# Moving half of the output projections' weight splits, the last differential head's units and the rotary copies

## The chip, the cores and the metric

The kernel runs on one core of a Trainium2 chip. The core has engines that run side by side, each with its own in-order stream of instructions: TensorE (PE) multiplies matrices, with its weight loads shown as PEld; VectorE (DVE), ScalarE (ACT) and GpSimd (POOL) work on tiles; SyncE (SP) mainly issues DMA transfers. They wait for each other by semaphores. The metric is the device time of one execution in microseconds (us); lower is better. A time is the median of several executions of the same program.

## The reference, cut to what matters

The whole program is a trunk of two layers over 1024 tokens of 1024 features, all in float32. Each layer is a token mixer and a gated MLP with a short convolution. Layer 0 mixes by differential attention (8 heads, two score maps each, partial rotary), layer 1 by multi-head latent attention, MLA (16 heads, with one rotary key that all heads share).

```python
for i in range(DEPTH):                       # DEPTH = 2
    h = rms_norm(x, attn_norm_g[i])
    if i % N_MIXERS == 0:
        x = x + diff_attention(h, ...)       # ends in: o.reshape(b, s, D_MODEL) @ w_o
    else:
        x = x + mla_attention(h, ...)        # ends in: o.reshape(b, s, ...) @ w_o
    h = rms_norm(x, ffn_norm_g[i])
    x = x + conv_ffn(h, ...)
return rms_norm(x, final_norm_g)
```

In MLA the score of a head is a product over 64 own features plus one over 32 rotary features, whose key `k_pe` is the same for all 16 heads:

```python
sc = (jnp.einsum('bqhd,bkhd->bhqk', qn, k_nope)
      + jnp.einsum('bqhr,bkr->bhqk', qp, k_pe)).astype(jnp.float32) * scale
```

## The kernel before

**Split operands.** Every float32 product is done as three products of rounded halves: an operand x is split into a high part (a rounding copy, `hi`, L123 to 127) and a low part (x minus the high part, `lo`, L129 and 130). `mm3` (L117 to 121) issues high times low, high times high and low times high, so three matmuls stand for one. `hi` runs on ACT (L127) unless DVE is named (L125); `lo` runs on DVE unless POOL is named. `fetch` (L132) starts a DMA of a raw block into the next place of a ring, and `split` (L138) makes the two parts of a block.

**Order.** The code is written as a program for all engines. When the kernel is built, a scheduler of the framework puts the instructions of each engine into an order of its own, by dependences and a model of durations; the engine then runs them in that fixed order. So an edit at one place can move instructions far from it.

**Attention.** Both mixers run in steps (`steps`, L277). A step t handles one pair of query blocks of one head. It issues the score matmuls of its own pair, then the "units" of the step (pieces of the q, k and v projections of a later head or of the other half of the tokens), the transposes and the value product of step t - 1, and its own softmax. In layer 0 (`diff_attention`, L307) there are 32 steps, four to a head. A unit is (head, which, half), which is 0 for Q, 1 for K and 2 for V; K and V of the second half of the tokens stand in a head's first step, Q in its second, and the next head's first halves follow. Units of layer 0 take one bank of PSUM, "u", in turn, and 24 matmuls each. The o of a finished head goes to DRAM (`o_d`, stored at L1464 in layer 0 and L1513 in MLA).

**Output projection.** `project_first` (L459) computes o times the first four row blocks of w_o for all eight token tiles and adds it to x; `project_rest`, after it, does the last four. Each piece of o is read back from DRAM (`project`, L443; the DMA at L448), split, and multiplied: two groups of 12 matmuls to a token tile. In layer 0 the first four token tiles put their groups into the one bank "u" and are added at L472, the rest use the two-bank tiles "S" and are added at L477. In layer 0 these raw pieces of o go through the same ring (the two halves of s13) as the raw weights.

**The weights of it.** `prefetcher`, in the body of the kernel, gives a function `step` that each step of the last head (layer 0), or of the last ten steps (MLA), calls: it splits the row blocks that were fetched by the last call, low parts by turns on POOL and DVE, and fetches the next two. `finish` does so until all eight are split, ahead of `project_first`. In layer 0 the split blocks go to s0 to s7.

**The rotary copies.** A key of MLA is held as a tile of 128 partitions, the lower 64 the head's own, the upper 64 the rotary part. There are four such tiles, used by turns. The rotary part is computed once into tile 0 (`rotary`), and copied to tiles 1, 2 and 3 by `share` (L1327, half a tile of tokens a call). In layer 1, tile 1's copies are made ahead of the steps, tiles 2 and 3 in the steps 1 and 2 (`prepare`, L1332); the odd tiles on DVE, tile 2 on ACT.

Further names of the profile: L248 is a transpose, L1403 and L1404 are the score matmuls of layer 0, L1418 its exponential, L1431 the difference of the two maps; L1487 is the exponential of MLA, L1507 and L1508 its value product, L1485 and L1486 its mask and maximum, L1493 and L149 the scaling of probabilities.

Of the kernel before, what the change touches and what calls it, by code (L numbers as in the profile page):

```python
# [18 lines left out]
P = 128  # L19
S = 1024  # L20
D = 1024
NT = S // P
KD = D // P
# [3 lines left out]
DA_HEADS = 8  # L27
# [29 lines left out]
class Trunk:  # L57
# [249 lines left out]
    def diff_attention(self, o_d, prefetch):  # L307
        nc, a = self.nc, self.a

        H = [[[self.at(f"s{4 * half + 2 * part + g}", [P, 4, 512], F32R) for g in range(2)] for half in range(2)] for part in range(2)]  # L310
        tab = self.at("s12", [P, 2, S])
        self.raw = self.ring(*self.cut("s13"))
        self.w = self.ring("s8", "s9", "s10", "s11")
        R = SimpleNamespace(
            k=self.ring("u0", "u1", "u2"), qh=self.ring("u3", "u4"), v=self.ring("u5", "u6", "u7"),
            P=self.ring("u8", "u9", "u10", "u11", "u12"), pT=self.ring("u13", "u14", "u15"),
            o=self.ring("h2", "h3"), fin=self.ring("h4", "h5", "h6", "h7"),
            rope=self.ring("h8", "h9", "h10", "h11"),
        )
# [12 lines left out]
        def split_w(h, which):  # L332
            if h < DA_HEADS:
                raw = raws.pop((h, which))
                w = self.w([P, 2, D], F32R)
                self.hi(w[:, 0, :], raw)
                self.lo(w[:, 1, :], raw, w[:, 0, :], nc.gpsimd)
                heads[h]["w", which] = w[:, 0, :], w[:, 1, :]


        def fetch_x(i):
            x = R.P([P, D])
            nc.sync.dma_start(x, a["x"][i * P : (i + 1) * P, :])
            return x

        def token_tile(i, x):
            r = self.rstd(x, self.big(), D)
            nc.vector.scalar_tensor_tensor(x, x, r, g, ALU.mult, ALU.mult)
            s = slice((i % 4) * P, (i % 4 + 1) * P)
            for kg in range(2):  # L350
                self.turn_blocks(x[:, kg * 512 : (kg + 1) * 512], lambda part: H[part][i // 4][kg][:, :, s])

        def unit(h, which, half):
            hd = heads[h]
            return self.da_unit(R, H, hd["w", which], which, half, hd, tab)

        xs = [fetch_x(0)]
        g = self.gain("s11", a["attn_norm_g"][0])
        xs += [fetch_x(1), fetch_x(2)]
        fetch_w(0, 1)  # L360
        xs += [fetch_x(3)]
        fetch_w(0, 0)
        nc.sync.dma_start(tab, a["rope_da"])
        split_w(0, 1)
        for i in range(4):
            token_tile(i, xs[i])
            if i == 1:
                self.load_constants()
        xs += [fetch_x(4), fetch_x(5), fetch_x(6)]
        fetch_w(0, 2)  # L370
        split_w(0, 0)
        self.run([unit(0, 1, 0)])
        split_w(0, 2)
        fetch_w(1, 1)
        self.run([unit(0, 0, 0)])
        for i in range(4, NT):
            if i + 3 < NT:
                xs += [fetch_x(i + 3)]
            token_tile(i, xs[i])
        self.run([unit(0, 2, 0)])  # L380

        def prepare(t):
            h, p = divmod(t, 4)
            if p == 0:
                split_w(h + 1, 1)
                fetch_w(h + 1, 0)
            if p == 1:
                split_w(h + 1, 0)
                fetch_w(h + 1, 2)
            if p == 2:  # L390
                split_w(h + 1, 2)
            if p == 3:
                fetch_w(h + 2, 1)
            if h + 1 == DA_HEADS:
                prefetch()

        def units(t):
            h, p = divmod(t, 4)
            todo = [[(h, 1, 1), (h, 2, 1)], [(h, 0, 1), (h + 1, 1, 0)], [(h + 1, 0, 0)], [(h + 1, 2, 0)]][p]
            return [unit(*u) for u in todo if u[0] < DA_HEADS]  # L400

        self.steps(lambda t: DaStep(self, R, *divmod(t, 4), heads, o_d), units, prepare, 4 * DA_HEADS)
# [53 lines left out]

        return into

    def project_first(self, W, o_d, os, x_src, at, early):  # L459

        nc = self.nc
        X = [None] * NT
        for q, pair in enumerate(self.PAIRS):
            for i in pair:
                X[i] = at(q, i)
                nc.sync.dma_start(X[i], x_src[i * P : (i + 1) * P, :])
                into = self.project(i, range(0, 4), W, o_d, os, self.raw)
                if q < early:
                    for b in (0, 512):
                        y = self.bank("u")  # L470
                        into(y, b)
                        nc.vector.tensor_add(X[i][:, b : b + 512], X[i][:, b : b + 512], y)  # L472
                else:
                    y = self.big()
                    for b in (0, 512):
                        into(y[:, b : b + 512], b)
                    nc.vector.tensor_add(X[i], X[i], y)  # L477
        return X

    def project_rest(self, W, o_d, os, X, at, x_d, g, junk, places, nat, more, begin):  # L480
# [752 lines left out]
    def mla_heads(self, cT, v_d, o_d):  # L1233
        nc, a = self.nc, self.a
        pairs = MLA_HEADS // 2
        heads = [dict() for _ in range(MLA_HEADS)]
        W, V, raws = {}, {}, {}
        w_places = [("u2", "u3"), ("u4", "u5")]
        v_ring, q_ring, t_ring = self.ring("s13", "s4"), self.ring("s1", "s10", "s5", "s9"), self.ring("h10", "h11", "h8")
        k_places, kT = ["s0", "s11", "s12", "s8"], []  # L1240
# [3 lines left out]
            P=self.ring("u6", "u7", "u8", "u9", "u12"), pT=self.ring("u0", "u1", "u10", "u11"), o=self.ring("h4", "h5", "h6", "h7"),  # L1244
# [82 lines left out]
        def share(j, half):  # L1327
            k_tiles(j + 1)
            s = slice(half * 512, (half + 1) * 512)
            self.hi(kT[j][64:128, :, s], kT[0][64:128, :, s], nc.vector if j % 2 else None)  # L1330

        def prepare(t):  # L1332
            p, u = divmod(t, 8)
            if t == 0:
                fetch_w(1)
            if t == 1:
                split_w(1)
                share(2, 0)
                share(3, 0)
            if t == 2:  # L1340
                share(2, 1)
                share(3, 1)
            for at, ahead, f in ((2, 1, fetch_v), (4, 1, split_v), (5, 2, fetch_w), (7, 2, split_w)):
                if u == at and p + ahead < pairs:
                    f(p + ahead)
            if t >= 4 * MLA_HEADS - 10:
                prefetch[0]()
# [171 lines left out]
def kernel_body(tc, a, out):  # L1519
    with ExitStack() as ctx:  # L1520
        k = Trunk(tc, ctx, a)
        nc = tc.nc
        k.constants()
        dram = lambda name, shape: k.dr.tile(shape, F32, name=name)
        o_d = [dram(f"o_d{l}", [KD, P, S]) for l in range(2)]
        v_d = dram("v_d", [KD, P, NT, P])
        x_d = [dram(f"x_d{l}", [S, D]) for l in range(3)]
        g_d = [dram(f"g_d{l}", [NF, P, S]) for l in range(2)]
        units = lambda *ids: [f"u{i}" for i in ids]
        slots = lambda *ids: [f"s{i}" for i in ids]  # L1530
        halves = lambda *ids: [f"h{i}" for i in ids]
# [10 lines left out]
            return [lambda: piece(0), lambda: piece(1)]  # L1542


        def prefetcher(w_o, W, places):

            raws = []

            def step():
                while raws:  # L1550
                    W.append(k.split(places[len(W)], raws.pop(0), nc.vector if len(W) % 2 else None))
                while len(W) + len(raws) < KD and len(raws) < 2:
                    i = len(W) + len(raws)
                    raws.append(k.fetch(w_o[i * P : (i + 1) * P, :], D))

            def finish():
                while raws or len(W) < KD:
                    step()

            return step, finish  # L1560


        W = []
        step, finish = prefetcher(a["da_w_o"], W, slots(*range(8)))
        k.diff_attention(o_d[0], step)
        finish()
        first = {}
# [3 lines left out]
                first[q] = k.cut(f"s{8 + q}")  # L1571
            return first[q][i // 4]

        X = k.project_first(W, o_d[0], k.ring(*k.cut("s12", 512)), a["x"], at, 2)
        k.raw = k.ring("u14", "u15")
        pl = SimpleNamespace(
            T=dict(B11=slots(0, 1), B21=slots(2, 3), B22=slots(8, 9), T1=slots(12, 13), T2=slots(10, 11), T3=slots(4, 5), T4=slots(6, 7)),
# [7 lines left out]
        more = SimpleNamespace()  # L1585
# [69 lines left out]
        k.raw = k.ring("u14", "u15")  # L1655
        heads = k.mla_input(W_in, hts, turns, v_d, lambda cT: k.mla_heads(cT, v_d, o_d[1]))
        W = []
        step, finish = prefetcher(a["mla_w_o"], W, slots(2, 3, 6, 7, 1, 10, 0, 11))
        heads.rest(step)
        finish()  # L1660
        places = iter(units(2, 3, 4, 5, 12, 13, 10, 11))
        X = k.project_first(W, o_d[1], k.ring(*halves(0, 1, 2, 3)), x_d[1], lambda q, i: k.at(next(places), [P, D]), 0)
        pl = SimpleNamespace(
            T=dict(B11=slots(4, 9), B21=slots(12, 8), B22=slots(5, 13), T1=slots(6, 7), T2=slots(2, 3), T3=slots(10, 11), T4=slots(0, 1)),
            w=units(6, 7, 9, 8, 2, 3), sums=halves(9, 10, 11, 3, 8, 0), tmp=halves(1, 2, 4, 5, 6, 7), u=units(0, 1, 12, 13), t=units(10, 11),
# [112 lines left out]
```

## Time and profile before

| what | value |
|---|---|
| median of 3 executions | 2463.72 us (2462.08 to 2464.77) |
| profiled execution | 2467.78 us |
| its span, first to last instruction | 2466.0 us |
| mean granted clock of TensorE | 0.991 |

The profile is of one execution, with every instruction's start and length. A page sums it up; views of it show the busy time of each engine by windows, the timeline of an engine with what released it, and groups of like instructions. Matmuls overlap, so a matmul's own length (some 0.39 us for 512 columns) is longer than the distance to the next. "Clock" is the share of its full clock that TensorE was granted in a stretch.

The places that the change touches lie in the span like this: the last head of layer 0 from about 450 us, the start of the MLA steps at about 1365 us, and the last ten of them from about 1600 us.

### The profile page before, as it was taken

The page shows a single profiled execution, that of the slowest core. Times are in us where ns is not written, and L with a number is a line of the kernel's source. Part 1 is how long each engine was busy: PE and PEld are TensorE (multiplying, and loading weights), DVE is VectorE, ACT ScalarE, POOL GpSimd, SP SyncE. Part 2 cuts the span into 40 slices and gives each one's busy share as a digit, 9 for nine tenths or more (in the row PEclk, how much of TensorE's full clock was granted, in tenths as well). Part 3 has the DMA queues.
Part 4 walks back from the last instruction along what each step waited for, and adds up shares of the span by engine and source line. Part 5 has one row for each costly group of instructions (what it writes and reads, how often), then busy time and mean ns, then how long its engine had stood idle before and what let it go on. Part 6 is the DMA issues. An engine that isn't in the chain of part 4 may idle for free.

```text
span 2466.0 us, 32632 instructions
## 1 busy us (share of the span) xinstructions
PE 2380.1 (97%) x11960; PEld 2014.0 (82%) x11960; DVE 1906.0 (77%) x3088; ACT 1299.6 (53%) x2428; POOL 642.5 (26%) x507
## 2 busy tenths in 40 slices
PE   7999999899999999999999999999999999999998
PEld 5888887788888888788899788887888888887886
DVE  6667776846888888899864877776378888888997
ACT  5677777744444444444444777776244444444443
POOL 5545554525100000000042566655340000000001
PEclk9999999899999999999999999999999999999999
DMA  4111111313222222543222111123222222227501
GB/s 158 40 35 44 35 35 44 124 60 120 70 93 77 86 77 93 194 163 125 83 88 68 52 40 39 39 66 113 95 91 79 86 77 89 82 81 277 167 5 77
DMA packets 95104, 213.91 MB, mean 87 GB/s; under 512 B 8672, under 2 KB 33888, under 8 KB 94816
## 3 DMA queue, kind: packets, MB, share of 16 engines
q1 hardware_dynamic: 86048, 184.56, 22.8%
q10 hardware_dynamic: 8896, 27.27, 3.0%
q8 instruction: 94, 1.54, 0.3%
q14 instruction: 66, 0.54, 0.1%
HBM read 159.37 MB, written 52.43 MB: 86 GB/s over the span
## 4 chain that ended last, share of the span: by engine, by line
PE 80%; DVE 7%; ACT 5%; issue 3%; POOL 2%; DMA 2%; SPq 0%; ACTq 0%; POOLq 0%; DVEq 0%
PE S L119 13%; PE S L120 13%; PE S L121 13%; PE b L119 8%; PE b L121 8%; PE b L120 8%; PE u L119 3%; PE u L120 3%; PE u L121 3%; PE b L248 2%; PE b L182 1%; ACT u L1418 1%; PE u L1508 1%; PE u L1507 1%; ACT u L127 1%
## 5 line engine op out<-in xcount | busy, mean ns | idle before, releaser
L163 POOL TENSOR_TENSOR st<-st,mhalf 128x1 f32<-128x1 f32 x56 | 32.5, 580 | 1305.9 <-DVE st L162 1302.0
L127 ACT CAST u<-h 128x512 fp32r<-128x512 f32 (+2 forms) x242 | 146.1, 619 | 283.1 <-DVE h L632 260.6
L119 PE MATMUL S<-s,u 128*128 128x512 f32 (+1 forms) x752 | 286.3, 381 | 1.7 <-DVE u L776 1.0
L121 PE MATMUL S<-s,u 128*128 128x512 f32 (+1 forms) x752 | 284.7, 379 | 0.0
L120 PE MATMUL S<-s,u 128*128 128x512 f32 (+1 forms) x752 | 284.7, 379 | 0.0
L119 PE MATMUL b<-s,u 128*128 128x512 f32 x588 | 231.6, 394 | 0.5
L120 PE MATMUL b<-s,u 128*128 128x512 f32 x588 | 229.8, 391 | 0.0
L121 PE MATMUL b<-s,u 128*128 128x512 f32 x588 | 229.7, 391 | 0.0
L689 DVE SCALAR_TENSOR_TENSOR u<-u,conv,u 128x1023 f32<-128x1023 f32 (+1 forms) x176 | 224.9, 1278 | 1.6 <-ACT u L685 1.6
L149 POOL TENSOR_TENSOR u<-u,st 128x384 f32<-128x384 f32 (+7 forms) x160 | 169.5, 1067 | 161.2 <-DVE st L1493 108.0
L119 PE MATMUL u<-s,s 128*128 128x512 f32 x448 | 183.1, 409 | 13.8 <-ACT h L416 6.7
L130 DVE TENSOR_TENSOR u<-b,u 128x512 fp32r<-128x512 f32 (+1 forms) x256 | 158.7, 631 | 38.9 <-ACT u L127 36.6
L121 PE MATMUL u<-s,s 128*128 128x512 f32 x448 | 177.4, 396 | 0.0
L120 PE MATMUL u<-s,s 128*128 128x512 f32 x448 | 177.0, 395 | 0.0
L127 ACT CAST s<-u 128x512 fp32r<-128x512 f32 (+4 forms) x197 | 123.5, 663 | 96.4 <-PE u L121 35.1
L119 PEld LDWEIGHTS S<-s,u 128*128 128x128 f32 x752 | 141.8, 189 | 29.8 <-issue 2.1
L120 PEld LDWEIGHTS S<-s,u 128*128 128x128 f32 x752 | 142.0, 189 | 26.1
L121 PEld LDWEIGHTS S<-s,u 128*128 128x128 f32 x752 | 142.0, 189 | 26.0
L127 ACT CAST u<-b 128x512 fp32r<-128x512 f32 (+1 forms) x256 | 133.9, 550 | 47.9 <-PE b L248 44.3
L692 ACT ACTIVATE u<-u 128x1024 f32<-128x1024 f32 x44 | 46.7, 1062 | 198.8 <-DVE u L689 198.8
L248 PE MATMUL b<-ident,u 128*128 128x128 f32 x864 | 138.5, 278 | 8.5 <-DVE u L130 5.7
L130 DVE TENSOR_TENSOR u<-h,u 128x512 fp32r<-128x512 f32 x166 | 114.1, 687 | 32.4 <-ACT u L127 31.5
(257 smaller groups left out, 6635.4 us busy)
## 6 DMA issues: line engine op xcount, KB each, us to landing
u<-in_ffn_up SPq DMA_DIRECT2D x88, 512.0 KB, 3.9
g_d<-u ACTq DMA_DIRECT2D x44, 512.0 KB, 2.6
u<-in_ffn_down SPq DMA_DIRECT2D x66, 256.0 KB, 5.3
u<-g_d SPq DMA_DIRECT2D x62, 256.0 KB, 4.6
s<-in_da_wqkv SPq DMA_DIRECT2D x24, 512.0 KB, 3.7
x_d<-u SPq DMA_DIRECT2D x16, 512.0 KB, 2.9
s<-x_d SPq DMA_DIRECT2D x8, 1024.0 KB, 9.2
u<-o_d SPq DMA_DIRECT2D x24, 256.0 KB, 2.9
```

Source lines behind the costliest of these rows:

```text
L119: mm(out, lh, rl, start=first, stop=False, skip_group_check=onto)
L120: mm(out, lh, rh, start=False, stop=False, skip_group_check=onto)
L121: mm(out, ll, rh, start=False, stop=last, skip_group_check=onto)
L127: self.nc.scalar.copy(out, src)
L130: (eng or self.nc.vector).tensor_sub(out, src, hi.bitcast(F32))
L149: self.nc.gpsimd.tensor_mul(x, x, s.to_broadcast(list(x.shape)))
L163: nc.gpsimd.tensor_tensor(r, s, self.mhalf, ALU.pow)
L182: self.nc.tensor.transpose(ps[:, k * P : (k + 1) * P], src[:, k * P : (k + 1) * P], self.ident)
L248: self.nc.tensor.transpose(ps[:, j * P : (j + 1) * P], probs[t][:, k : k + P], self.ident)
L689: nc.vector.scalar_tensor_tensor(t[half][:, back:], u[half][:, : S - back], w, t[half][:, back:], ALU.mult, ALU.add)
L692: nc.scalar.activation(t[0], t[0], AF.Silu)
L1418: nc.scalar.activation(e, sc[c], AF.Exp, bias=nm[:, c : c + 1], accum_out=l[:, c : c + 1])
```

## The change

Three edits. `prefetcher` splits only the first four row blocks ahead of `project_first`. `finish` then issues the DMAs of the other four into places of their own, which the attention's probabilities held (u10 to u13 in layer 0, u6 to u9 in layer 1), and `project_first` calls `rest`, one split with its low part on DVE, after each of the token tiles 0 to 3. In layer 0's last head, the units K, Q and V of the second half of the tokens stand in one step each, in this order. In MLA, all rotary copies run on ACT, and those of tiles 2 and 3 are asked for one half tile a step in the steps 3 to 6.

```diff
         def units(t):
             h, p = divmod(t, 4)
             todo = [[(h, 1, 1), (h, 2, 1)], [(h, 0, 1), (h + 1, 1, 0)], [(h + 1, 0, 0)], [(h + 1, 2, 0)]][p]
+            if h + 1 == DA_HEADS:
+                todo = [[(h, 1, 1)], [(h, 0, 1)], [(h, 2, 1)], []][p]
             return [unit(*u) for u in todo if u[0] < DA_HEADS]
...
-    def project_first(self, W, o_d, os, x_src, at, early):
+    def project_first(self, W, o_d, os, x_src, at, early, more):
...
                     nc.vector.tensor_add(X[i], X[i], y)
+                if i < 4:
+                    more()
         return X
...
         def share(j, half):
             k_tiles(j + 1)
             s = slice(half * 512, (half + 1) * 512)
-            self.hi(kT[j][64:128, :, s], kT[0][64:128, :, s], nc.vector if j % 2 else None)
+            self.hi(kT[j][64:128, :, s], kT[0][64:128, :, s])
...
             if t == 1:
                 split_w(1)
-                share(2, 0)
-                share(3, 0)
-            if t == 2:
-                share(2, 1)
-                share(3, 1)
+                k_tiles(4)
+            if 3 <= t < 7:
+                share(2 + (t - 3) // 2, (t - 3) % 2)
...
-        def prefetcher(w_o, W, places):
+        def prefetcher(w_o, W, places, later):
...
+            half = KD // 2
 
             def step():
                 while raws:
                     W.append(k.split(places[len(W)], raws.pop(0), nc.vector if len(W) % 2 else None))
-                while len(W) + len(raws) < KD and len(raws) < 2:
+                while len(W) + len(raws) < half and len(raws) < 2:
                     i = len(W) + len(raws)
                     raws.append(k.fetch(w_o[i * P : (i + 1) * P, :], D))
 
             def finish():
-                while raws or len(W) < KD:
+                while raws or len(W) < half:
                     step()
-
-            return step, finish
+                for i, place in zip(range(half, KD), later):
+                    raws.append(k.at(place, [P, D]))
+                    nc.sync.dma_start(raws[-1], w_o[i * P : (i + 1) * P, :])
+
+            def rest():
+                if raws:
+                    W.append(k.split(places[len(W)], raws.pop(0), nc.vector))
+
+            return step, finish, rest
...
-        step, finish = prefetcher(a["da_w_o"], W, slots(*range(8)))
+        step, finish, rest = prefetcher(a["da_w_o"], W, slots(*range(8)), units(10, 11, 12, 13))
...
-        X = k.project_first(W, o_d[0], k.ring(*k.cut("s12", 512)), a["x"], at, 2)
+        X = k.project_first(W, o_d[0], k.ring(*k.cut("s12", 512)), a["x"], at, 2, rest)
...
-        step, finish = prefetcher(a["mla_w_o"], W, slots(2, 3, 6, 7, 1, 10, 0, 11))
+        step, finish, rest = prefetcher(a["mla_w_o"], W, slots(2, 3, 6, 7, 1, 10, 0, 11), units(6, 7, 8, 9))
```

In layer 1 `project_first` is given `rest` in the same way.

More of the change, by code (lines that the diff above doesn't have):

```diff
@@ L1661, in kernel_body @@
         places = iter(units(2, 3, 4, 5, 12, 13, 10, 11))
-        X = k.project_first(W, o_d[1], k.ring(*halves(0, 1, 2, 3)), x_d[1], lambda q, i: k.at(next(places), [P, D]), 0)
+        X = k.project_first(W, o_d[1], k.ring(*halves(0, 1, 2, 3)), x_d[1], lambda q, i: k.at(next(places), [P, D]), 0, rest)
         pl = SimpleNamespace(
```

## The prediction

> **What bounds the kernel now.** I read the page first (span, engines, chain of waits), then the busy time by windows around the three places that the diff touches, then the timelines of TensorE and of the engine that released it at each gap.
>
> ```profile
> span 2466.0 us, 32632 instructions
> PE 2380.1 (97%) x11960; PEld 2014.0 (82%) x11960; DVE 1906.0 (77%) x3088; ACT 1299.6 (53%) x2428; POOL 642.5 (26%) x507
> PE 80%; DVE 7%; ACT 5%; issue 3%; POOL 2%; DMA 2%; SPq 0%; ACTq 0%; POOLq 0%; DVEq 0%
> ```
>
> TensorE is busy for 97% of the span and is 80% of the chain that ends last. The change adds no matmul, so it can only win back time in which TensorE sits idle or runs at a lower clock, and it can only lose time by making more of that. So the question is where such time lies. The windows (columns: length, busy us of PE, PEld, DVE, ACT, POOL with counts, granted clock, DMA share, GB/s) show it: the first three lie in layer 0's last head, the next two at the start of the latent attention (MLA), the sixth is its long middle, then come its last steps, and the last is a stretch of layer 1's output projection.
>
> ```profile
> 450.00:460.00 10.00, 7.40 (x24) 5.69 (x25) 8.64 (x14) 7.68 (x15) 2.55 (x2) 0.83 0.56 206
> 470.00:480.00 10.00, 6.30 (x43) 5.19 (x41) 9.80 (x14) 7.08 (x18) 7.75 (x6) 0.88 0.68 236
> 480.00:490.00 10.00, 8.25 (x26) 6.84 (x27) 8.34 (x14) 8.46 (x20) 7.51 (x5) 0.50 0.18 54
> 1360.00:1370.00 10.00, 5.63 (x29) 4.23 (x27) 9.76 (x11) 6.03 (x8) 6.55 (x4) 0.93 0.52 157
> 1370.00:1380.00 10.00, 9.24 (x40) 7.67 (x40) 8.12 (x19) 7.12 (x15) 5.06 (x4) 0.73 0.08 19
> 1400.00:1640.00 240.00, 234.14 (x1506) 208.52 (x1505) 190.76 (x466) 176.72 (x388) 151.66 (x121) 1.00 0.14 41
> 1640.00:1650.00 10.00, 8.04 (x42) 6.87 (x41) 8.01 (x18) 6.97 (x15) 5.67 (x6) 0.83 0.30 88
> 1660.00:1670.00 10.00, 8.66 (x56) 7.38 (x55) 8.58 (x20) 8.74 (x19) 9.75 (x7) 1.00 0.71 229
> 1670.00:1680.00 10.00, 8.87 (x59) 7.24 (x58) 8.46 (x21) 7.67 (x17) 7.49 (x7) 1.00 0.52 175
> 1680.00:1690.00 10.00, 8.27 (x54) 7.28 (x54) 7.11 (x18) 7.06 (x16) 8.43 (x5) 1.00 0.29 84
> 1725.00:1755.00 30.00, 30.00 (x134) 24.80 (x133) 7.43 (x7) 3.73 (x6) 7.56 (x6) 1.00 0.22 66
> ```
>
> The last row gives the price of a 512-wide matmul at full clock, 30.00/134 = 0.224 us. In 470 to 480 TensorE is busy for 6.30 of 10 us while DVE is busy for 9.80: there DVE is the bound. In 480 to 490 the granted clock is 0.50, so half of 8.25 busy us are lost as well. Counting idle time plus the share of the clock that is missing, the three windows lose at most (2.60+1.7)+(3.70+1.2)+(1.75+4.1) = 15.1 us, the MLA start (4.37+0.4)+(0.76+2.5) = 8.0. That is all that there is to win at these places.
>
> **Part 1: the second half of the projection's weights goes out of the last head.** In layer 0, four 128x1024 row blocks lose their split there. What TensorE and DVE do around it (start, length, engine, instruction, idle time before and its releaser):
>
> ```profile
> 478.36 0.69 PE L248 MATMUL b<-ident,u 128*128 128x128 f32 x2 [1.70 <-DVE u L1431]
> 479.98 0.76 PE L1403 MATMUL S<-u,h 128*128 128x512 f32 x1 [0.94 <-ACT u L1418]
> 486.04 0.80 PE L1403 MATMUL S<-u,h 128*128 128x512 f32 x1 [1.60 <-ACT u L1418]
> 496.26 0.48 PE L1403 MATMUL S<-u,h 128*128 128x512 f32 x1
> 472.88 2.02 DVE L130 TENSOR_TENSOR s<-s,s 128x1024 fp32r<-128x1024 f32 x1
> 485.40 2.10 DVE L130 TENSOR_TENSOR s<-s,s 128x1024 fp32r<-128x1024 f32 x1
> L130 POOL TENSOR_TENSOR s<-s,s 128x1024 fp32r<-128x1024 f32 x28 | 69.1, 2467 | 48.8 <-ACT s L127 35.3 <-issue 11.6 <-DVE st L1428 1.8
> L127 ACT CAST s<-s 128x1024 fp32r<-128x1024 f32 x32 | 33.8, 1055 | 25.3 <-PE u L121 19.8 <-DVE u L348 2.6 <-DMA s<-in_da_w_o 2.6
> 483.90 8.81 SPq L448 DMA_DIRECT2D s<-o_d  x4
> DMA to landing us min/median/max: 3.6/4.0/6.2
> ```
>
> Removed from this stretch: 4 casts on ACT (4 x 1.06 = 4.2 us), two low parts on DVE (2.02 + 2.10 = 4.1) and two on POOL (2 x 2.47 = 4.9). The gaps of 1.70, 0.94 and 1.60 us end on DVE and ACT, the engines that are relieved. There is a second effect. The raw blocks no longer pass through the ring from which the o pieces are read, so the reads that waited on SP until 483.90 are issued earlier, and in the order of the built instructions four of the projection's first groups (48 matmuls) instead of one (12) stand ahead of the score that starts at 496.26. They fill the gaps: 36 x 0.224 = 8.1 us of work that TensorE has on hand while it waited.
>
> **Part 2** goes with this: Q comes before V, one unit a step. Its 72 matmuls, its rotary and transposes are the same in number; what moves is where they stand, by up to one step. That Q's score follows sooner is worth at most the 1.1 us by which the score could come at 495.2 when the two DVE low parts before it are gone, less what stands in the ring. So the ideal is 8.1 + 1.1 = 9.2 of the 15.1 lost. DVE, though, stays near its bound (9.80 less 2.02 in the worst window), so I take 7.7.
>
> Added are four DMAs of 512 KB on SP, four casts on ACT and four low parts, now all on DVE. The blocks are needed by the projection's second half, which begins about 545, and are split by about 516 if each lands 4.0 us after its issue: 29 us of cover, without which they would cost 4 x (1.06 + 2.1) = 12.6. The place where they can hurt is the order on ACT: the cast of block 4 stands ahead of the casts of two o pieces. Its DMA is issued when the last transposes have read the place that it goes to, lands 4.0 us later, and the casts take 1.06 and about 0.6; TensorE has 36 narrow matmuls between (half-width products, 36 x 0.11 = 4.0). The next projection group waits 4.0 + 1.06 + 0.6 - 4.0 = 1.7 us. Bounds: 0 if the place comes free sooner, 3.4 if the wait brings half a clock dip too. Layer 0: -7.7 + 1.7 = **-6** (from -11, ideal plus the second half of the half-clock time, to -2, the DVE bound).
>
> The low parts go to DVE just when POOL makes those of the o pieces. In the last row below, such a part of 1024 took 2.25 us with POOL at work, and in the group's mean 1.32. The Trainium skill, "GPSIMD Engine Reference", section "1. Specifications", says that POOL shares its interface to SBUF with DVE where two inputs come from SBUF; that speaks against the change, and the trace agrees. By it the four parts cost 4 x 0.93 = 3.7 us more on DVE; the sum stays, since DVE has 22.6 of 30 us free in the projection's window.
>
> ```profile
> L130 DVE TENSOR_TENSOR s<-u,s 128x1024 fp32r<-128x1024 f32 x10 | 13.2, 1324 | 2.3 <-ACT s L127 2.3
> 1666.24 2.25 DVE L130 TENSOR_TENSOR s<-u,s 128x1024 fp32r<-128x1024 f32 x1
> ```
>
> **Part 1 in layer 1.** The same edit at the end of the MLA:
>
> ```profile
> 1641.14 1.05 ACT L127 CAST s<-u 128x1024 fp32r<-128x1024 f32 x1 [1.74 <-DMA u<-in_mla_w_o]
> 1643.53 0.50 PE L119 MATMUL S<-s,s 128*128 128x512 f32 x1 [1.71 <-ACT u L1487]
> 1668.97 0.36 PE L1507 MATMUL u<-u,s 128*128 128x256 f32 x1 [1.06 <-DVE st L1493]
> 1671.11 1.18 PE L248 MATMUL b<-ident,u 128*128 128x128 f32 x7 [0.45 <-POOL u L149]
> 1675.46 0.50 PE L119 MATMUL S<-s,s 128*128 128x512 f32 x1 [0.62 <-ACT u L1487]
> 1683.05 0.38 PE L1507 MATMUL u<-u,s 128*128 128x256 f32 x1 [0.96 <-DVE h L1511]
> ```
>
> At 1641.14 ACT, in order, waits 1.74 us for a weight's DMA with the exponentials of the next step behind it, and TensorE misses those for 1.71 us; the clock then falls to 0.83 in that window (10 x 0.17 = 1.7). In the built order that cast now stands behind two exponentials, so both go: 3.4. The four later stalls (1.06 + 0.45 + 0.62 + 0.96 = 3.1) lie among the splits of blocks 4 to 7, which leave. Together 6.5; other DVE work is late next and takes a part of it, so **-4.5** (bounds -1, if only half the first stall goes, and -7).
>
> The Trainium skill, "TensorE: Matmul & The Clock Gate", section "HAM oscillation — how this bites in real kernels", wants a gap of over some 3.4 us for the half clock. By that rule the dip at 1643 is not the gap's doing and the sum would be 1.7 less; the rows differ, with clocks of 0.83 and 0.50 behind gaps of 1.71 and 1.70.
>
> **Part 3: rotary copies at the MLA start.**
>
> ```profile
> 1365.30 1.04 ACT L127 CAST s<-s 64x1024 fp32r<-64x1024 f32 x1
> 1366.37 0.48 ACT L127 CAST u<-b 128x384 fp32r<-128x384 f32 x1
> 1364.98 3.40 DVE L125 CAST s<-s 64x1024 fp32r<-64x1024 f32 x2
> 1368.41 0.56 DVE L130 TENSOR_TENSOR u<-b,u 128x384 fp32r<-128x384 f32 x1
> 1369.03 0.58 PE L1507 MATMUL u<-u,s 128*128 128x256 f32 x1 [4.13 <-DVE u L130]
> ```
>
> TensorE's longest gap here, 4.13 us, ends on DVE's low part at 1368.41, which stood behind the two copies of 3.40 us. They leave DVE. In the built order ACT has three copies one behind the other where it had one, so its 384-wide cast comes 2 x 1.04 = 2.1 us later, at about 1368.5, unless what is before them also comes earlier; DVE's low part follows it. The copies are thus not really spread: the order of the instructions hoists them. Between 3.40 gained on DVE and the delay on ACT, and with the clock of 0.73 in the next window (2.5 us) partly won back, I take **-3** (bounds 0, ACT takes DVE's place in full, and -6, the gap goes with its dip).
>
> The change also reorders the instructions of all 64 MLA steps. Nothing is added there. The long middle window has 240 - 234.14 = 5.9 us idle at clock 1.00, so it cannot win over 5.9; I take 0, with ±4.
>
> **Sum.** -6 - 3 - 4.5 + 0 = -13.5. The profiled execution took 2467.78 us (span 2466.0 and 1.8 around it), 4.1 above the median of the runs shown: 2454.3 for it, and 2463.72 - 13.5 = **2450** for a median.
>
> **The rivals.**
>
> *The DVE and ACT chains stay the bound.* For it: DVE at 9.80 of 10 in 470 to 480, and 8.34 after. Then the projection's early matmuls fill gaps, but the last scores come no sooner. Layer 0 gives only -2, the MLA tail -2, the start -1.5: 2458.
>
> *The copies only change engines.* If ACT is as late as DVE was, the MLA start gives 0 and the rest stands: 2453. For it: the three copies stand back to back. Against it: DVE is at 9.76 of 10 in 1360 to 1370, ACT at 6.03.
>
> *More is won.* If early projection work also takes the place of the half-clock time in 480 to 490, layer 0 gives its -11, and the tail its -6: 2463.72 - 20 = 2444.
>
> *Slower: the new order of the MLA steps.* One mechanism: in the middle window a step's exponential or low part falls behind another step's on its engine, and TensorE stalls as at 1643.53, for 1.71 us and 1.7 of lower clock, 3.4 each. Four such stalls eat the 13.5, and more than that decide for slower; six cost 20.4 and give 2463.72 + 6.9 = 2471. For it: every engine's order is changed there. Against it: 1506 matmuls with 2.4% idle at clock 1.00, ACT at 74% and DVE at 79%.
>
> **How the numbers follow.** A measurement of this kernel can tell about 0.2%, 4.9 us. The forecast (2445 to 2455, its own range) has 0.50; copies that only change engines 0.13, which lies in that range as well; the chains that stay 0.17, of which 0.10 counts as faster (below 2458.8) and 0.07 as the same; more won 0.08; slower order 0.12, of which 0.02 ends within 0.2% and 0.10 above. So faster is 0.81, same 0.09, slower 0.10. The parts' bounds give -11 - 6 - 7 = -24 at the far end and -2 - 0 - 1 = -3 at the near one, that is 2440 to 2461; with a part of the middle's ±4 the range is 2438 to 2464, which leaves out most of the slower case.
>
> **What would show it.** Right: in layer 0 four projection groups before the last head's last scores, no clock of 0.50 over ten us, and the projection starting some 6 us sooner; at the MLA start a gap of about 1 to 2 us where 4.13 was; at 1640 no ACT wait on a DMA of a weight; the middle window as busy as now. Wrong: a TensorE gap that ends on a cast of blocks 4 to 7 of over 2 us, DVE or ACT at over 95% in the last head with the same gaps, new stalls among the MLA steps, or a second half of the projection that waits for a low part.

## The result and the profile after

The changed kernel takes 2442.51 us (median of 6, 2441.41 to 2444.52) where the kernel before took 2463.30 us (median of 6, 2462.08 to 2465.87). The ratio is 0.9911, with a 95% interval of 0.9901 to 0.9921: 20.8 us less, 0.9%. The forecast was 2450, its range 2438 to 2464.

The profiled execution took 2441.99 us. Its page:

```profile
span 2440.2 us, 32668 instructions
PE 2365.8 (97%) x11960; PEld 2003.9 (82%) x11960; DVE 1905.3 (78%) x3088; ACT 1303.3 (53%) x2432; POOL 630.4 (26%) x503
```

TensorE has the same 11960 matmuls. The windows of the changed kernel, chosen like those of before and moved with the shift (columns: length, busy us of PE, PEld, DVE, ACT, POOL with counts, granted clock, DMA share, GB/s):

```profile
450.00:460.00 10.00, 7.24 (x27) 5.43 (x26) 8.65 (x14) 7.69 (x14) 2.55 (x2) 0.83 0.46 157
470.00:480.00 10.00, 10.00 (x62) 8.92 (x61) 8.62 (x15) 7.25 (x23) 6.60 (x7) 1.00 0.54 184
480.00:490.00 10.00, 10.00 (x58) 8.59 (x57) 7.31 (x15) 8.80 (x19) 3.02 (x3) 1.00 0.10 28
1350.00:1360.00 10.00, 6.98 (x36) 5.21 (x34) 8.72 (x13) 8.60 (x12) 6.61 (x4) 1.00 0.47 150
1360.00:1370.00 10.00, 8.30 (x43) 7.14 (x44) 7.63 (x18) 7.93 (x18) 6.09 (x4) 0.83 0.13 43
1390.00:1630.00 240.00, 236.73 (x1536) 211.90 (x1535) 196.81 (x482) 180.90 (x400) 156.79 (x125) 1.00 0.15 43
1660.00:1670.00 10.00, 10.00 (x71) 9.19 (x71) 9.12 (x23) 7.85 (x18) 6.26 (x4) 1.00 0.12 28
1670.00:1680.00 10.00, 9.77 (x79) 9.20 (x78) 8.80 (x26) 8.67 (x21) 6.46 (x6) 1.00 0.24 67
```

From 470 to 490 TensorE is now busy throughout, at full clock, where it had 14.55 of 20 us and a clock of 0.50 in the second half. Four of the projection's groups of 12 matmuls now stand ahead of the score at 496.25, where one stood ahead of the score at 496.26; the last head's last score comes at 500.34, 5.0 us sooner. The window at 450 is about as it was. In the long middle of the MLA steps TensorE does 30 more matmuls in the same 240 us. The last windows are nearly full.

How far this moves the work is best read from the starts of the same instruction in both traces. I use four landmarks: the first exponential of MLA (L1487 before), the value products (L1507) at one sixteenth and at eleven sixteenths of their number, and the last value product. The differences between them give each stage's own change against the profile of before, in us. The medians come from four sessions, in which the kernel before itself read 2463.3 to 2465.4; kernels of different sessions are compared by their ratios to before.

| kernel | median | layer 0, to the first exponential | MLA start | middle | last steps | TensorE's loss in the middle |
|---|---|---|---|---|---|---|
| before | 2463.3 | 0 | 0 | 0 | 0 | 11.0 |
| changed | 2442.5 | -10.7 | -2.8 | -4.3 | -7.0 | 5.5 |
| part 1 alone | 2459.9 | -3.9 | 0.0 | +0.1 | -4.9 | 11.0 |
| part 2 alone | 2462.2 | -3.2 | -0.5 | 0.0 | -2.3 | 11.0 |
| part 3 alone | 2452.8 | +0.2 | -1.8 | -5.9 | -6.7 | 4.2 |
| parts 1 and 2 | 2453.1 | -10.5 | -0.8 | +0.1 | -6.4 | 10.9 |
| parts 1 and 3 | 2449.8 | -4.0 | -2.2 | -3.7 | -7.0 | 6.1 |
| changed, no early groups | 2456.5 | -4.8 | -0.2 | 0.0 | -6.0 | 10.9 |
| tile 1 on ACT, 2 and 3 on DVE | one time | -2.4 | -0.3 | +0.1 | -2.3 | 10.9 |
| tiles 1 and 2 on ACT, 3 on DVE | one time | -2.7 | -0.4 | +0.1 | -2.4 | 10.9 |
| changed, tile 3 on POOL, splits later | 2449.4 | -9.9 | -2.8 | 0.0 | -4.1 | 10.9 |
| changed, high parts on DVE | 2442.0 | -13.3 | -2.5 | -6.2 | -5.4 | 3.9 |
| changed, all eight tiles through u | 2453.2 | -2.7 | -2.7 | -4.2 | -6.6 | 5.5 |
| high parts on DVE, tiles 2 and 3 on POOL | 2444.2 | -9.0 | +1.5 | -9.3 | -5.4 | 2.3 |

The last column is worked out from the traces: for each matmul of the middle the distance to the next one's start, less the price of its width at full rate (0.2265 us for 512 columns, about 0.1 for 128), added up where it is over 0.1 us.

The profiled execution of before took 2467.78 us, 4.5 above its median, and the table shows where. Three kernels whose last steps stand in the very order of before (part 2 alone, and the two with other copies) show -2.3 to -2.4 in that column; the four that leave layer 0 alone, before among them, show 0, +0.2, -2.4 and -2.7 in the first, -1.2 in the mean. In the same order, TensorE stood at half clock for 23.9, 23.9, 20.5 and 13.7 us of their layer 0, which goes some way to explain the differences. Part 2 alone shows -0.5 at the MLA start, which it doesn't touch. Taken from these zeros, the changed kernel wins about 9.5 us in layer 0, 2.3 to 2.8 at the MLA start, 4.3 in the middle and 4.7 in the last steps, in all some 21, against 20.8 by the medians. The columns are good to one or two us only, since the order around a landmark is not the same in all kernels: priced by width, the changed kernel has 0.9 us less matmul work ahead of the first exponential than before, 0.4 less in the MLA start, 0.3 more in the middle and 1.7 more before the last value product.

The steps that the prediction named show in these lines. First two gaps of TensorE that are left (start, length, engine, instruction, idle time before and its releaser), then ACT around them, then DVE:

```profile
524.87 0.50 PE L121 MATMUL S<-s,s 128*128 128x512 f32 x1 [1.14 <-POOL s L130]
1360.24 0.39 PE L1509 MATMUL u<-u,s 128*128 128x256 f32 x1 [2.28 <-DVE h L1513]
```

```profile
521.38 1.05 ACT L127 CAST s<-u 128x1024 fp32r<-128x1024 f32 x1 [2.61 <-DMA u<-in_da_w_o]
1355.84 2.94 ACT L127 CAST s<-s 64x1024 fp32r<-64x1024 f32 x3
1358.80 0.48 ACT L127 CAST u<-b 128x384 fp32r<-128x384 f32 x1
1359.31 0.37 ACT L1512 COPY h<-u 64x256 f32<-64x256 f32 x1
```

```profile
525.30 1.85 DVE L130 TENSOR_TENSOR s<-u,s 128x1024 fp32r<-128x1024 f32 x1 [0.48 <-ACT s L127]
1359.79 0.40 DVE L1513 TENSOR_TENSOR h<-h,u 64x256 f32<-64x256 f32 x1
```

At 521.38 ACT waits 2.61 us for the DMA of block 4, the cast of an o piece is behind it, then POOL's low part, and TensorE misses it for 1.14 us. At 1355.84 the three rotary copies run one behind the other for 2.94 us; the copy of L1512 stands behind them, DVE's L1513 behind that, and TensorE waits 2.28 us. This is not the wait of 4.13 made shorter. That one stood ahead of the second value product, where 0.42 us are left; the 2.28 stand ahead of the third, which had no gap before.

The 3.40 us that the two copies took on DVE before are not their own cost either. One took 2.79 us, the other 0.69, and the long one ran beside this instruction of POOL:

```profile
1364.88 2.34 POOL L130 TENSOR_TENSOR u<-u,u 128x1024 fp32r<-128x1024 f32 x1 [0.46 <-ACT u L127]
```

### The profile page after: what moved, and what is told of

The parts are those of the page before. It is cut to its first block, busy times and chain, and to the rows that moved or that the text cites. A ratio compares the mean times of both kernels' runs of the same rounds, so it can differ in the third digit from the quotient of the medians.

```text
span 2440.2 us, 32668 instructions
## 1 busy us (share of the span) xinstructions
PE 2365.8 (97%) x11960; PEld 2003.9 (82%) x11960; DVE 1905.3 (78%) x3088; ACT 1303.3 (53%) x2432; POOL 630.4 (26%) x503
## 4 chain that ended last, share of the span: by engine, by line
PE 81%; DVE 7%; ACT 4%; issue 3%; DMA 2%; POOL 2%; SPq 0%; POOLq 0%; ACTq 0%; DVEq 0%
PE S L119 13%; PE S L120 13%; PE S L121 13%; PE b L119 8%; PE b L120 8%; PE b L121 8%; PE u L119 4%; PE u L120 3%; PE u L121 3%; PE b L248 3%; PE u L1510 1%; PE u L1509 1%; PE b L182 1%; ACT u L1420 1%; PE S L1405 1%
```

## The experiments

**The parts, alone and in pairs.** Each kernel takes the whole lines of the change that belong to its part and leaves the others as they were. Without part 3, for instance:

```diff
-                k_tiles(4)
-            if 3 <= t < 7:
-                share(2 + (t - 3) // 2, (t - 3) % 2)
+                share(2, 0)
+                share(3, 0)
+            if t == 2:
+                share(2, 1)
+                share(3, 1)
```

Part 1 alone, in both layers:

> Only part 1 (second half of the weights split beside the projection, both layers). The built order of the MLA steps up to the last ones is that of before. Theory (splits are what crowds the last head and the MLA tail): layer 0 wins about 7 of its 10 us and the tail about 8.5, in all -13 to -16 us against before. Rival (the unit order is what frees layer 0, and part 3's new order is what frees the tail): layer 0 wins 0 to 2, the tail 3 to 4, in all -3 to -6.

Measured: 2459.94 us against 2464.65, ratio 0.9980 (0.9971 to 0.9989), -4.7. A miss; the total is in the rival's range, -3 to -6. Layer 0 did win early on: the last add of the projection's first half came 12.1 us sooner than in the profile of before. Then it gave most of it back. TensorE of this kernel, followed by SP's DMA issues:

```profile
538.41 0.40 PE L1461 MATMUL b<-h,ones 128*128 128x512 f32 x1
550.85 0.80 PE L119 MATMUL S<-s,h 128*128 128x512 f32 x1 [6.79 <-ACT h L127]
```

```profile
544.14 0.33 SPq L1466 DMA_DIRECT2D o_d<-h  x1
545.90 6.63 SPq L448 DMA_DIRECT2D u<-o_d  x3
```

The projection's second half needs the o of the last head. That head's end is late: its sum of squares (L1461) runs at 538.41, its o is stored at 544.14 (before: 538.85) and read back from 545.90 on, and TensorE waits 6.79 us for the cast of it. The early projection work had filled the gaps of the last head, and the gap came back behind it.

Part 2 alone:

> Only part 2 (Q before V, one unit a step, in the last head of layer 0); MLA as before. Theory: as the eight splits stay in the head, it is within 2 us of before, and TensorE's gaps on DVE and the half clock near 480 stay. Rival: the order of the units alone wins 6 us or more, without those gaps.

Measured: 2462.16, ratio 0.9989 (0.9980 to 0.9997), -2.5. That is half a microsecond past the theory's 2 us: with eight splits in the head the order of the units is worth little. The gaps on DVE stay, as it said (2.63 us at 480.17), but the half clock near 480 does not: the clock is 1.00 from 470 to 490.

Part 3 alone:

> Only part 3 (rotary copies on ACT, asked for in steps 3 to 6); layer 0 as before. Theory: the MLA start wins 3.5 us and the middle up to 3, the last steps nothing: -3 to -6. Rival 1: the new order also frees the last steps, -10 or more. Rival 2: the middle's gain is noise of the order, -1 to -3.

Measured: 2452.78, ratio 0.9953 (0.9940 to 0.9965), -11.9. The theory falls and rival 1 holds: this part, whose edits lie in the first steps, wins 5.9 us in the middle and about 4.4 in the last steps, and only 1.8 at the place that it touches.

Parts 1 and 2:

> Parts 1 and 2 without 3. Theory (parts add, 1 and 2 help each other in layer 0): -15 to -18 against before, with the MLA start's gap of 4.1 us still there. Rival (the tail's gain needs part 3): -10 to -12, with stalls in the last ten MLA steps.

Measured: 2453.09, ratio 0.9953 (0.9939 to 0.9966), -11.6. The theory missed, and the total is the rival's, but not for the rival's reason: the last steps win nearly as much as with part 3 (-6.4 against -7.0), and what is missing is the middle (+0.1 against -4.3). Parts 1 and 2 alone add up to 7.2, so together they win 4.4 more; layer 0 shows it, -10.5 against -3.9 and -3.2. The MLA start has its old gap:

```profile
1358.63 0.39 PE L1511 MATMUL u<-u,s 128*128 128x256 f32 x1 [4.13 <-DVE u L130]
```

Parts 1 and 3, to see whether part 2 takes away the wait for the last head's o:

> Parts 1 and 3 without part 2 (K and V in one step, then Q). The middle's order is the changed kernel's. Theory (part 2 brings the last head's own end forward, without it the projection's second half waits for the store and the load of the last head's o, 6.8 us as in part 1 alone): 6 to 7 us slower than the changed kernel, a gap of 6 us or more released by a cast of o near 550. Rival (parts add, part 2 is worth its own 2.5): 2 to 3 slower, no such gap.

Measured: 2449.77, ratio 0.9937 (0.9923 to 0.9950), by the ratios 6.4 us slower than the changed kernel; layer 0 alone loses 6.7. The theory holds, and the wait is there again:

```profile
551.40 0.79 PE L119 MATMUL S<-s,h 128*128 128x512 f32 x1 [6.82 <-ACT h L127]
```

In the changed kernel, with Q in front, SP stores the last o and reads it back about 5 us sooner, and no TensorE gap stands there (whether Q ahead of V or one unit a step does it was not tried apart):

```profile
538.99 0.33 SPq L1466 DMA_DIRECT2D o_d<-h  x1
541.02 5.07 SPq L450 DMA_DIRECT2D u<-o_d  x2
```

**Early projection groups.** One argument of `project_first` says how many pairs of token tiles go through bank u. At 0 they use the tiles that the scores need too, and can't stand ahead of the last scores.

```diff
-        X = k.project_first(W, o_d[0], k.ring(*k.cut("s12", 512)), a["x"], at, 2, rest)
+        X = k.project_first(W, o_d[0], k.ring(*k.cut("s12", 512)), a["x"], at, 0, rest)
```

> The changed kernel, but layer 0's first projection groups use the two-bank tiles S (which the scores need too) in place of bank u, so that they can't stand ahead of the last scores; splits and unit order are the changed kernel's. Theory (the groups that stand ahead fill TensorE's gaps): layer 0 loses 6 to 9 us of its 10, gaps released by ACT and DVE are back between 470 and 505, the total is -11 to -15 against before. Rival (the relief of ACT and DVE alone does it): within 2 us of the changed kernel, -19 to -22.

Measured: 2456.45, ratio 0.9964 (0.9951 to 0.9977), -9.0, less than the theory's -11 to -15. Layer 0 loses 5.9 us of its 10.7, just below the forecast, and TensorE waits for ACT and DVE as before, though the splits are out of the way:

```profile
477.85 0.39 PE L119 MATMUL b<-u,u 128*128 128x256 f32 x1 [2.37 <-DVE u L130]
487.40 0.80 PE L1405 MATMUL S<-u,h 128*128 128x512 f32 x1 [2.22 <-ACT u L1420]
```

So the relief of DVE and ACT alone is the smaller half; the groups on hand fill the gaps. The total fell by more than layer 0 did, because the MLA steps of this kernel came out in the order of before: see below.

**All eight tiles through bank u** (4 in place of 2 in the same argument):

> The changed kernel with all eight token tiles of layer 0's first half through bank u (16 groups that can stand ahead of or between the last scores, where 8 did). The middle's order is the changed kernel's. Theory (TensorE has no long gap left in the last head after 460): nothing more is won there, -1 to +1 against the changed kernel. Rival (more groups ahead fill more): -2 to -3.

Measured: 2453.17, ratio 0.9950 (0.9938 to 0.9963), by the ratios 9.6 us slower than the changed kernel. Both expectations missed. With one bank for all, groups wait for the add of the one before (three TensorE gaps of 0.46 to 0.96 us, of which the changed kernel has the first), and then the second half's transposes wait, for longer than in the three together. Why they come late was not taken apart:

```profile
567.67 1.12 PE L182 MATMUL b<-ident,h 128*128 128x128 f32 x4 [3.92 <-POOL h L495]
```

**Order or load in the MLA steps.** Two kernels change only which engine copies which tile, against the kernel before:

```diff
-            self.hi(kT[j][64:128, :, s], kT[0][64:128, :, s], nc.vector if j % 2 else None)
+            self.hi(kT[j][64:128, :, s], kT[0][64:128, :, s], nc.vector if j > 1 else None)
```

> The kernel before with the copies of tile 1 on ACT, and those of tiles 2 and 3 on DVE: as many copies on DVE (4) and ACT (2) as before, in another built order of the MLA steps. Theory (the order alone decides the middle): time that TensorE loses over 0.1 us a matmul in the middle of the MLA steps, 11.0 us in every kernel with before's order, is another here, by 2 us or more either way. Rival (the load of DVE decides): 10 to 12.

> The kernel before with tile 1's copies on ACT, tile 3's still on DVE: half of the engine change of part 3, in a third order. Theory (order alone): the middle's loss is a number of its own, not midway between 11.0 and part 3's 4.2. Rival (load): 7 to 8.5. At the MLA start the gap of 4.13 us is under 1.5 in both, since one or no copy stands ahead of DVE's low part.

(The second has `j == 3` there.) One time each, 2462.32 and 2464.75, near before. Both lose 10.9 us in the middle. The load rival's number for the first came true and for the second didn't (7 to 8.5). The theory's condition was not met either: the middle of their built order turned out to be before's, row for row (1363 TensorE rows between the landmarks), so neither had an order of its own. And the gaps at the start are 3.99 and 3.53, not under 1.5: one copy on DVE is enough when it stands beside POOL (2.76 us in the second kernel).

```profile
1365.78 0.58 PE L1507 MATMUL u<-u,s 128*128 128x256 f32 x1 [3.53 <-DVE u L130]
```

What settles it is the last column of the table beside the built orders. Eight kernels have before's order in the middle, and all lose 10.9 or 11.0 us there, whatever engine makes the copies; among them the one without early groups, which has part 3 in full. The copies themselves can't act there: in every kernel they are over more than 20 us before the middle begins. The order of part 3 alone and of the kernel with high parts on DVE loses 4.2 and 3.9; that of the changed kernel 5.5, 5.5 and 6.1. The waits of TensorE in the middle (what waited, for whom: us, times, longest) of before, of the kernel without early groups, and of the changed kernel:

```profile
PE b L248 <- DVE u L130: 4.2, 8, 0.9
```

```profile
PE b L248 <- DVE u L130: 4.1, 8, 0.8
```

```profile
PE b L248 <- DVE u L130: 1.1, 2, 0.9
```

In before's order a transpose waits eight times, by turns 0.18 and 0.86 us, for a bank that a low part on DVE still reads; in the other orders it mostly doesn't. By the measure of the table's last column these waits are 5.6 of the 11.0 us before and 1.5 of the 5.5 in the changed kernel; the rest of the loss is spread over many small steps. Over the middle of both, of the kernel without early groups and of part 3 alone, TensorE is busy for 97.6% and 98.9% of the middle, and DVE does more in the second, not less:

```profile
1396.00:1607.00 211.00, 205.85 (x1328) 183.21 (x1327) 166.98 (x408) 155.24 (x342) 133.96 (x107) 1.00 0.13 38
```

```profile
1397.00:1609.00 212.00, 209.73 (x1369) 188.71 (x1367) 172.95 (x422) 160.54 (x351) 142.24 (x112) 1.00 0.13 38
```

The built orders show one thing more, by building alone (these two were not run). A kernel with only the spread of the copies over steps 3 to 6 has, on all five engines, the very order of before, and one with only the move to ACT has that of part 3. The scheduler hoists the copies wherever they are asked for.

**Attempts at more.** First tile 3's copies on POOL, and blocks 4 to 7 split after token tiles 4 to 7:

```diff
-            self.hi(kT[j][64:128, :, s], kT[0][64:128, :, s])
+            (nc.gpsimd.tensor_copy(kT[j][64:128, :, s], kT[0][64:128, :, s]) if j == 3 else self.hi(kT[j][64:128, :, s], kT[0][64:128, :, s]))
...
-                if i < 4:
+                if i >= 4:
                     more()
```

> The changed kernel with two further edits in separate places: tile 3's rotary copies on POOL, and the splits of blocks 4 to 7 after the token tiles 4 to 7 in place of 0 to 3. Theory: of the three copies of 2.94 us on ACT at the MLA start one or two leave, the gap of 2.28 us behind them falls under 1; the wait of 1.14 us at 524.87 in layer 0, behind block 4's cast, goes: -2 to -4 against the changed kernel, give or take 3 from the new order of the steps. Rival (POOL's copies delay its scaling of probabilities, and the blocks come late for the second half): 0 to +4.

Measured: 2449.36, ratio 0.9930 (0.9914 to 0.9947), by the ratios 4.7 us slower than the changed kernel, about the rival's +4, though the two intervals overlap. The middle fell back into before's order (4.3 us), the gap at the start was still 1.75, and block 4's cast was hoisted to where it had been, with the same 1.14 us of waiting behind it.

Then the high parts of blocks 4 to 7 on DVE, which takes that cast out of ACT's order by force:

```diff
-                    W.append(k.split(places[len(W)], raws.pop(0), nc.vector))
+                    raw, w = raws.pop(0), k.at(places[len(W)], [P, 2, D], F32R)
+                    k.hi(w[:, 0, :], raw, nc.vector)
+                    k.lo(w[:, 1, :], raw, w[:, 0, :], nc.vector)
+                    W.append((w[:, 0, :], w[:, 1, :]))
```

> The changed kernel, but the high parts of blocks 4 to 7 are made on DVE like their low parts, so that no cast that waits for a weight's DMA stands in ACT's order. Its MLA steps come out in the order of part 3 alone, whose middle lost 4.2 us. Theory: the wait of 1.14 us at 524.87 goes, the middle loses 4 to 4.5 in place of 5.5, DVE (under 50% busy there) takes the four copies (about 1.2 us each) without harm: -1 to -3 against the changed kernel, -22 to -24 against before. Rival (the adds that free bank u wait behind DVE's weights): a new gap of over 1 us released by the add, 0 to +2.

Measured: 2441.99, ratio 0.9909 (0.9894 to 0.9925). Against the changed kernel's 0.9911 that is no difference that can be told. The mechanism is as expected: no wait near 524.87, DVE waits for the weights instead, in time that it has, and the middle loses 3.9.

```profile
521.72 0.69 DVE L125 CAST s<-u 128x1024 fp32r<-128x1024 f32 x1 [1.97 <-DMA u<-in_da_w_o]
```

Last, the same with tiles 2 and 3 copied on POOL:

> The changed kernel with the high parts of blocks 4 to 7 on DVE and the rotary copies of tiles 2 and 3 on POOL (tile 1's on ACT). Its MLA steps have a fourth order, which shares 1133 of 1277 rows of the middle with part 3's alone. Theory: the middle loses 4 to 5.5 (order); at the MLA start the gap of 2.28 us behind ACT's three copies falls under 1, as ACT keeps one: -2 to -5 against the changed kernel, 2438 to 2441. Rival (POOL needs over 1.5 us a copy and holds up its scaling of the probabilities): a gap of over 1.5 us released by POOL at the MLA start, and no gain.

Measured: 2444.17, ratio 0.9918 (0.9904 to 0.9931). The middle's loss is the lowest of all, 2.3 us, but the MLA start is 4.3 us worse than the changed kernel's (+1.5 and -2.8 in the table). A part of both is work that moved: there is 1.5 us less of it in this middle than in before's and 0.7 more in the start than in the changed kernel's. POOL is not slow, two copies take 2.37 us; the gap only falls to 1.45, because DVE now has a maximum and a low part of its own ahead of the add that TensorE waits for. What else the start loses was not taken apart. POOL first, then DVE:

```profile
1357.27 2.37 POOL L1334 CAST s<-s 64x1024 fp32r<-64x1024 f32 x2
```

```profile
1359.41 1.09 DVE L1488 TENSOR_REDUCE st<-S 128x1 f32<-128x896 f32 x1
1360.41 0.55 DVE L130 TENSOR_TENSOR u<-b,u 128x384 fp32r<-128x384 f32 x1
1360.88 0.40 DVE L1513 TENSOR_TENSOR h<-h,u 64x256 f32<-64x256 f32 x1
```

No version beat the changed kernel beyond its interval.

## Why the prediction was right, and where its sizes were off

The sign, the range and three of the places held; the forecast's own band (2445 to 2455) was 2.5 us too high, and the rival "more is won" (2444) came closest. The fourth place, the middle, was put at nothing either way and gave a fifth of the gain; that it fell on the fast side was luck. Without it the total would lie at about 2447, inside the band.

- **Layer 0, -6 forecast, about -9.5 measured.** The term that was mis-sized is the shading of the ideal 9.2 to 7.7 because "DVE stays near its bound": DVE fell from 9.80 to 8.62 of 10 us and TensorE ran full, so the ideal was reached whole, as far as a column good to one or two us can tell. The wait behind block 4's cast, put at 1.7, is there with 1.14 us, through the chain that was described; that it is this cast is shown by the kernel without it on ACT.
- **What carries layer 0** was put wrongly between parts. Part 2 was given at most 1.1 us; taking it out costs 6.4. The prediction looked at the gaps before the last scores and not at what the last head's own end sets free: its o, which the second half of the projection reads back. With early groups ahead of it that end becomes the next bound, and Q in front brings it forward. The early groups themselves, priced at 8.1 for three more than before, are worth 5.9 in layer 0 by the kernel that has none ahead.
- **The cover of blocks 4 to 7** was put at 29 us. The second half began at about 541, and block 7's low part ended at 525.30 + 1.85 = 527.15: 14 us, still enough. Of the four low parts only this one, begun while POOL was at work, took 1.85; the others took 1.21 to 1.23. So the slowdown that the prediction took from the Trainium skill, "GPSIMD Engine Reference", section "1. Specifications" (VectorE and GpSimd share their interface to SBUF when a VectorE instruction has two inputs there), came to 0.6 us in place of 3.7.
- **The MLA start, -3 forecast, -2.3 to -2.8 measured,** of which 0.4 is work that moved. The first half of the mechanism held: the copies leave DVE, they are hoisted together, and ACT comes late behind them. The path from there was another. The cast at 1366.37 that the prediction delays is not the one that the low part at 1368.41 reads; that is the 384-wide cast before it, at 1363.38, which no copy holds up. So the gap of 4.13 all but went, to 0.42, and a new one came one value product later, behind DVE's add L1513 and ACT's copy L1512. That its 2.28 us lie near the forecast's "1 to 2" is luck. The two copies were read as 3.40 us of DVE's work; about 1.4 is theirs, as 0.69 is what the others took, and the rest is the time that one stood beside POOL. The rival in which ACT gives all of it back did not hold, though the kernel without early groups, with the same copies and a gap of 2.33, wins only 0.2 here, with 0.9 us more work ahead of its landmark; what else it loses is open.
- **The middle, 0 ± 4 forecast, -4.3 measured,** a little outside. The prediction said that every order changes there and gave it no sign. It bounded the gain by the 5.9 us idle of the window of 234.14 of 240 busy us. TensorE's loss by the distances was 11.0 in the 218 us between the landmarks, since a matmul's own length counts as busy, and it is longer than the distance that it needs; the last kernel brought it down to 2.3. The slower rival was the same idea with the other sign.
- **The last steps, -4.5 forecast, about -4.7 measured,** but not for the forecast's reason alone: part 1 by itself wins about 2.6 there, part 3's order by itself about 4.4, both together 4.7.

That the loss in the middle follows the order and not the load is shown by kernels of equal order with the copies on different engines, all of them over before the middle begins. Why the scheduler falls into one order or another after a distant edit is open: it was seen, not tried apart.

## What to carry to other kernels

Work that is moved ahead to fill an engine's gaps wins only if the chain that follows is not the next bound: look up who reads the result of the work that now stands behind it (here a store and a load of the last head's o, 6.8 us). Where a scheduler fixes the order, compare the built orders before explaining a difference: an edit can be nothing in the order (the spread over steps) or reorder steps far away (the copies' engine), and a stall that comes back at each step shows as a waiter with a count. A window at 97% busy can still hold several microseconds.

## What the hardware showed unexpectedly

Equal orders lose nearly equal time in the middle, where the clock is full in every kernel: the eight profiles with before's order agree within 0.1 us of 11. The two with part 3's order lose 4.2 and 3.9, the three with the changed kernel's 5.5, 5.5 and 6.1. So differences of about a microsecond in such a stretch can be read from one trace, smaller ones not.

The lower clock does not follow from the gap's length alone. The window from 450 to 460 has two gaps; with 1.31 and 1.44 us (high parts on DVE) the clock stayed 1.00, with 1.32 and 1.44 (changed) it fell to 0.83, which is half clock for 3.41 us in the trace. High parts on DVE, its window and its gaps:

```profile
450.00:460.00 10.00, 7.25 (x34) 5.78 (x34) 8.65 (x14) 7.68 (x15) 2.56 (x2) 1.00 0.47 159
```

```profile
451.33 0.50 PE L1405 MATMUL S<-u,h 128*128 128x512 f32 x1 [1.31 <-ACT u L1420]
453.96 0.50 PE L119 MATMUL u<-s,s 128*128 128x512 f32 x1 [1.44 <-DVE h L234]
```

The changed kernel's gaps there:

```profile
452.05 0.50 PE L1405 MATMUL S<-u,h 128*128 128x512 f32 x1 [1.32 <-ACT u L1420]
454.68 0.63 PE L119 MATMUL u<-s,s 128*128 128x512 f32 x1 [1.44 <-DVE h L234]
```

A rounding copy of 128x1024 took 0.69 us on DVE (at 521.72 above) and 1.05 on ACT (at 521.38 above). One of 64x1024 took DVE 0.69 too, and 2.79 when it began at 1364.98, just behind POOL's subtract of 1364.88 to 1367.22 in the kernel before. The two kernels with other copies show the same: 2.76 and 2.84 us for one begun just behind a POOL subtract, 0.69 for each of the others. A mean over the two copies of such a row, 1.70 us, is the cost of neither.
